# A two-layer hybrid diffusion backbone: modulation closes at raised priority, output-weight splits at a shorter spacing, half an output tile ahead of the last attention unit's close

## The chip, the cores and the metric

The kernel runs on one core of a Trainium2 chip. The metric is the device time of one execution in microseconds (us). The core has five engines that run side by side, each through its own queue of instructions: TensorE (PE; its weight loads are listed apart as PEld), VectorE (DVE), ScalarE (ACT), GpSimd (POOL) and SyncE (SP), which issues all of this kernel's DMAs. Semaphores order work between engines.

## What is computed

The reference is two layers over 1024 latent and 256 context tokens of width 1024. Each layer modulates a normalised input, projects it once, sends the columns through three groups of heads, and joins them in one output projection:

```
mod = silu(c) @ w_ada[l] + b_ada[l]              # shift, scale, gate
h   = rmsnorm(x, norm_g) * (1 + scale) + shift   # the same for the context
... = split(h @ w_in)
a   = gated delta rule, both directions, 4 heads of 128   # recurrence over tiles
b   = softmax attention, 4 heads, 10 key tiles of 128     # latent reads context + latent
c   = short gated convolution
x   = x + gate * (concat(a, b, c) @ w_out)       # the context too in the first layer
```

After the second layer only the 1024 latent tokens remain, and a last RMSNorm gives the output.

## The kernel before

Tokens are cut into ten tiles of 128 (eight latent, two context). Matrix products whose operands need more than one float32r pass are written as hi and lo parts, so a product is three passes: hi x hi, lo x hi, hi x lo. `split` (L74) makes such a pair: ScalarE copies the raw tile into hi, VectorE or POOL subtracts it to give lo.

**Order of the work.** Two things set it. First, the program issues its instructions through a small planner, `Sched` (L86): generators ("lanes") yield a delay, and `tick` moves the planner's clock and resumes the lanes that are due. The clock is advanced by estimates in the code, for example `sch.tick(0.0014 * n)` after each score product of n columns. `until(cond)` ticks by 1.0 until a condition holds. Second, the compiler then schedules each engine's queue by priority, which follows the order of issue, and by a model of when operands are ready; `tc.high_priority(offset=k)` issues as if k instructions earlier. Between L1279 and L1456, `tc.manual_schedule` keeps PE's instructions in the order of issue; the other engines stay free, and PE work issued after the region may still be placed between.

**Buffers.** Tiles come from tagged pools with a fixed number of buffers (L55). The change touches `P2` (7 buffers: `wr`, `ot2`, `za`, `zb`, `tm` and others), `T5` (5: `probT`, `xt`), `P4` and `B16` (7 large ones: among them the two halves of the output weights).

**Modulation.** `Ada` (L177) loads `w_ada`, multiplies it with the conditioning column, and `close` (L197) copies the product out of PSUM on ScalarE into `ms`, lets PE sum it over partitions (L209), and adds bias and scale on VectorE into A2 and B2 (L216, L218), which every modulated tile `hm` (L280) reads. For the first layer the closes stand at the very start; the others run as a lane beside the input projection.

**Attention.** The loop over `units` (group of queries, pair of heads) does five steps of two key tiles each (one step for the context group). A step issues scores (`a_scores`), exponentials into `probT` on ScalarE, sums of `probT` into `vt` on POOL (L1129; the last step's on VectorE, L1127, for the first head, and for both in the last unit), and the product with the values (`a_pv`, L1159). `a_out` (L1162) closes a unit: PE sums `vt` over partitions (L1170, "sum product"), VectorE takes the reciprocal (L1173) and scales, POOL multiplies by the gate, SP writes `bx_d`.

**Output.** When both directions of the recurrence are done, the lane `load_wo` (L1311) loads the output weights in two column halves of eight slices of 128 rows each: per slice a buffer `wr`, a DMA, a delay, a `split`, a delay (`load_wo_half`, L1324). `finish(i)` (L1332) treats one tile of tokens in four stages: load `ot2`, `raw` and `za`; the norm's statistics and the scaling of `ot` (L1344 to L1349); four transposes (L1353), scaling (L1354) and the split into `mix`, with the load of `xt`; and the output product, two column halves of 24 matmuls each (L84), with residual and gate on VectorE. `ahead(q)` (L1388) moves tiles q-2, q-1 and q on by one stage. `ahead(0)` and `ahead(1)` are called inside the last attention units, `ahead(2)` after the last value product; then come the last close, and a loop that calls `ahead(q)` and the output product of tile q-3.

Of the kernel before, what the change touches and what calls it, by code (L numbers as in the profile page):

```python
# [10 lines left out]
ALU = mybir.AluOpType  # L11
# [17 lines left out]
def kernel(  # L29
# [39 lines left out]
    V, A, P, T, S = nc.vector, nc.scalar, nc.gpsimd, nc.tensor, nc.sync  # L69
# [8 lines left out]
    def copy_a(out, in_):  # L78
        A.activation(out=out, in_=in_, func=ACTF.Copy)  # L79
# [41 lines left out]
    sch = Sched()  # L121
# [55 lines left out]
    class Ada:  # L177
# [18 lines left out]

        def close(self, third, q, pm, brow=None):  # L197
            ms = st([128, 256], "sm", name="ms")
            copy_a(ms, pm[:, 0:256])
            yield 3.0  # L200
            pc = bank()
            if third == 2:
                T.matmul(pc[0:32, 0:256], lhsT=csum, rhs=ms, start=True, stop=True)
                V.tensor_tensor(out=brow, in0=pc[0:2, 0:256], in1=brow, op=ALU.add)
                S.dma_start(out=self.y["gate"][:, 256 * q:256 * q + 256], in_=brow)
                return
            p3 = pc[:, 0:4].rearrange("p (b t) -> p b t", b=2)
            for b in range(2):
                T.matmul(p3[:, b], lhsT=ms[:, 128 * b:128 * b + 128], rhs=csum[:, 0:2], start=True, stop=True)  # L209
            out = self.y["A2" if third else "B2"][:, :, 2 * q:2 * q + 2]  # L210
            cols = self.y["col"]

            def row(c0):
                return cols[:, c0 + 2 * q:c0 + 2 * q + 2].unsqueeze(1).to_broadcast([128, 2, 2])

            V.tensor_tensor(out=out, in0=p3.rearrange("p b t -> p t b"), in1=row(78 + 8 * third), op=ALU.add)  # L216
            if third:
                V.scalar_tensor_tensor(out=out, in0=out, scalar=1.0, in1=row(60), op0=ALU.add, op1=ALU.mult)  # L218

        def lane(self):  # L220
            todo = [(t, q, k4) for t in self.thirds for q in range(4) for k4 in range(2)]
# [94 lines left out]
    for l in range(DEPTH):  # L316
# [603 lines left out]
        if l == 0:  # L920
# [16 lines left out]
            for t in (0, 1):  # L937
                for hf in range(2):
                    pms = [bank(), bank()]
                    for k4 in range(2):  # L940
                        for j in range(2):
                            q = 2 * hf + j
# [381 lines left out]
        def load_wo_half(q, wh, wl):  # L1324
            for k in range(KD):
                wr = st([128, 512], "P2", name="wr")
                S.dma_start(out=wr, in_=w_out[l, 128 * k:128 * k + 128, 512 * q:512 * q + 512])
                yield 1.5
                split(wr, wh[:, k], wl[:, k], P if k % 2 else V)
                yield 1.5  # L1330

        def finish(i):  # L1332
            raw = st([128, KD, 128], "P4", name="raw")
            ot = st([128, 4, 128], "P2", name="ot2")
            za = st([128, 4, 128], "P2", name="za")
            S.dma_start(out=ot, in_=o_d[i])
            S.dma_start(out=raw[:, 4:6, :], in_=bx_d[:, :, i * 128:(i + 1) * 128].rearrange("b p t -> p b t"))
            S.dma_start(out=raw[:, 6:8, :], in_=cx_d[:, :, i * 128:(i + 1) * 128].rearrange("b p t -> p b t"))
            S.dma_start(out=za, in_=za_d[:, :, i * 128:(i + 1) * 128].rearrange("b p t -> p b t"))
            yield 3.0  # L1340
            so = st([128, 4], "st", name="so")
            jk = st([128, 128], "h5", name="jk4")
            for h in range(4):
                A.activation(out=jk, in_=ot[:, h], func=ACTF.Square, accum_out=so[:, h:h + 1])  # L1344
            V.scalar_tensor_tensor(out=so, in0=so, scalar=1.0 / 128, in1=s_2[:, :, i], op0=ALU.mult, op1=ALU.mult)
            P.tensor_scalar(so, so, 1.0, EPS, ALU.mult, ALU.add)
            P.tensor_tensor(so, so, nhalf[:, 0:4], ALU.pow)
            V.tensor_tensor(out=so, in0=so, in1=s_1[:, :, i], op=ALU.mult)
            V.tensor_tensor(out=ot, in0=ot, in1=bc(so, 128), op=ALU.mult)  # L1349
            yield 3.0  # L1350
            pt = bank()
            for h in range(4):
                T.transpose(pt[:, h * 128:(h + 1) * 128], ot[:, h], ident)  # L1353
            V.scalar_tensor_tensor(out=raw[:, 0:4, :], in0=pt.rearrange("p (h f) -> p h f", h=4), scalar=col[:, 74:75], in1=za,  # L1354
                                   op0=ALU.mult, op1=ALU.mult)
            mix = st([128, 2, KD, 128], "W8", F32R, name="mix")
            split(raw[:, 0:4], mix[:, 0, 0:4], mix[:, 1, 0:4])
            split(raw[:, 4:8], mix[:, 0, 4:8], mix[:, 1, 4:8], P)
            xt = load_x(l, i)
            done[i] = xt  # L1360
            yield 3.5
            for q in range(2):
                pw = bank()
                wh, wl = wo[q]
                mm3(pw, [(mix[:, a_, k], w_[:, k]) for a_, w_ in ((0, wh), (1, wh), (0, wl)) for k in range(KD)])
                cs = slice(512 * q, 512 * q + 512)
                tm = st([128, 512], "P2", name="tm")
                V.tensor_tensor(out=tm, in0=pw, in1=gates[0 if i < NX else 1][:, cs], op=ALU.mult)
                V.tensor_tensor(out=xt[:, cs], in0=xt[:, cs], in1=tm, op=ALU.add)
                if last:  # L1370
                    if q == 0:
                        sf = st([128, 2], "st", name="sf")
                    A.activation(out=tm, in_=xt[:, cs], func=ACTF.Square, scale=D ** -0.5, accum_out=sf[:, q:q + 1])
            if not last:
                S.dma_start(out=xs_d[i], in_=xt)
                return
            V.scalar_tensor_tensor(out=sf[:, 0:1], in0=sf[:, 0:1], scalar=EPS, in1=sf[:, 1:2], op0=ALU.add, op1=ALU.add)
            P.tensor_tensor(sf[:, 0:1], sf[:, 0:1], nhalf[:, 0:1], ALU.pow)
            for q in range(2):
                cs = slice(512 * q, 512 * q + 512)  # L1380
                V.scalar_tensor_tensor(out=xt[:, cs], in0=xt[:, cs], scalar=sf[:, 0:1], in1=gates[1][:, cs], op0=ALU.mult, op1=ALU.mult)
                S.dma_start(out=out[0, i * 128:(i + 1) * 128, cs], in_=xt[:, cs])
# [69 lines left out]
        Q.clear()  # L1452
        ahead(2)
        sch.tick(2.0)
        next(ending)
        in_order.__exit__(None, None, None)  # L1456
        sch.tick(1.8)
        sch.until(lambda: wof.ok(0))
        for q in range(3, n_act + 3):
            ahead(q)  # L1460
            next(fg[q - 3], None)
            if q < n_act + 2:
                sch.tick(10.4)
            if last:
                continue
            if q > n_act:
                zpre.append(split_w(zr))
            if n_act <= q < n_act + 2:
                zr = load_w(l + 1, O_ZA + 128 * (q - n_act))
            if q == n_act + 2:  # L1470
                wof.put(1)
            sch.add(h_lane(act[q - 3], l + 1))
# [76 lines left out]
```

## Time and profile before

| | us |
|---|---|
| median of 3 runs | 1717.27 (1715.24 to 1718.92) |
| profiled execution | 1723.55 |
| its span, first to last instruction | 1721.8 |
| PE busy | 1650.5 |
| DVE busy | 1101.9 |
| ACT busy | 758.8 |
| POOL busy | 646.3 |

The table is to be read by stages. The share of an engine is a mean over stages with different limits; the number to look for is where PE stands idle or runs at its lower clock (the granted clock is given as a share of full speed: 1.00 is 2.4 GHz, 0.50 is 1.2 GHz). In the timeline a row gives the start, the duration, the engine, the line, the operation with its output and inputs, and in brackets the idle time before it and what ended that. Layer 0 ends its attention at about 803 us of the span, layer 1 at about 1614 us.

### The profile page before, as it was taken

Reading aid. Unit: us, or ns where it says so; the run is one execution under the profiler, and the core shown is the slowest. Engines: PE = TensorE matmul, PEld = TensorE weight load, DVE = VectorE, ACT = ScalarE, POOL = GpSimd, SP = SyncE. Lnnn points to the kernel's source line nnn. Section 1 sums busy time; section 2 is a strip of 40 time slices with the busy share of each in tenths; the row PEclk is TensorE's granted clock in tenths of the full one; section 3 lists DMA queues with packets and bytes.
Section 4 is the critical chain, followed back from the end, with each engine's and each line's share of the span. In section 5 each row is a group of like instructions: output and inputs, shape, how many; then the busy total and the mean of one; then the engine's idle time right before and its main releaser. Section 6 shows DMA issues by size and latency. Waiting matters only on the chain.

```text
span 1721.8 us, 29896 instructions
## 1 busy us (share of the span) xinstructions
PE 1650.5 (96%) x10964; PEld 1316.9 (76%) x10964; DVE 1101.9 (64%) x2041; ACT 758.8 (44%) x1909; POOL 646.3 (38%) x848
## 2 busy tenths in 40 slices
PE   7999999999999999998999999999999989999998
PEld 5887888787887877764888887787778778776586
DVE  2534668878643767765565346689797377776664
ACT  4644565223444534344354435652245444434432
POOL 0520345321320456557331212544232136556731
PEclk8999999999999899999999999999999989999999
DMA  9332464753254755544443314556524465454551
GB/s 360 124 126 79 155 196 150 242 178 123 78 160 125 257 157 177 186 144 159 132 141 111 104 56 134 161 179 224 166 70 128 151 211 164 160 188 156 172 159 49
DMA packets 195403, 266.54 MB, mean 155 GB/s; under 512 B 50529, under 2 KB 115249, under 8 KB 195257
## 3 DMA queue, kind: packets, MB, share of 16 engines
q1 hardware_dynamic: 195256, 264.64, 47.8%
q8 instruction: 87, 1.43, 0.3%
q14 instruction: 60, 0.48, 0.1%
HBM read 182.71 MB, written 79.17 MB: 152 GB/s over the span
## 4 chain that ended last, share of the span: by engine, by line
PE 68%; DVE 10%; DMA 9%; issue 5%; ACT 3%; POOL 3%; SPq 1%; POOLq 0%; DVEq 0%; ACTq 0%
PE bank L452 26%; PE bank L84 22%; PE bank L1159 3%; PE bank L1236 2%; PE bank L1255 2%; PE bank L1249 2%; DVE pr L680 2%; PE bank L1254 2%; PE bank L1102 2%; DMA gcb<-row_d 2%; DVE Mb L681 1%; DMA wa<-in_w_ada_dram 1%; PE bank L1226 1%; DVE acc L466 1%; PE bank L516 1%
## 5 line engine op out<-in xcount | busy, mean ns | idle before, releaser
L452 PE MATMUL bank<-h_hi,w 128*128 128x512 f32 x1664 | 432.5, 403 | 2.4 <-DVE h_hi L283 2.4
L452 PEld LDWEIGHTS bank<-h_hi,w 128*128 128x128 f32 x1664 | 305.4, 190 | 74.6 <-issue 4.5
L452 PE MATMUL bank<-h_lo,w 128*128 128x512 f32 x832 | 217.7, 402 | 0.0
L452 PEld LDWEIGHTS bank<-h_lo,w 128*128 128x128 f32 x832 | 154.3, 189 | 37.0 <-issue 1.6
L466 DVE SCALAR_TENSOR_TENSOR acc<-pad,col,acc 128x1284 f32<-128x1284 f32 (+1 forms) x104 | 160.1, 1540 | 11.1 <-ACT acc L463 9.5
L1129 POOL TENSOR_TENSOR vt<-vt,probT 128x512 f32<-128x512 f32 x110 | 144.7, 1335 | 20.2 <-ACT probT L1143 19.5
L84 PE MATMUL bank<-wo_hi,mix 128*128 128x512 f32 x576 | 145.0, 402 | 1.8 <-ACT wo_hi L75 1.1
L1143 ACT ACTIVATE probT<-bank 128x512 f32<-128x512 f32 (+1 forms) x168 | 96.5, 590 | 98.2 <-PE bank L84 92.2
L84 PEld LDWEIGHTS bank<-wo_hi,mix 128*128 128x128 f32 x576 | 108.2, 191 | 28.6 <-ACT wo_hi L75 2.6
L76 DVE TENSOR_TENSOR w<-wr,w 128x1024 fp32r<-128x1024 f32 x52 | 66.6, 1283 | 93.3 <-ACT w L75 93.3
L1104 DVE TENSOR_REDUCE mx<-bank 128x1 f32<-128x512 f32 (+1 forms) x200 | 108.5, 585 | 10.9 <-PE bank L1102 9.7
L452 PE MATMUL bank<-h_c,w 128*128 128x256 f32 x816 | 109.7, 287 | 0.0
L452 PEld LDWEIGHTS bank<-h_c,w 128*128 128x128 f32 x816 | 102.2, 190 | 5.8 <-issue 3.7
L75 ACT ACTIVATE w<-wr 128x1024 fp32r<-128x1024 f32 x52 | 54.9, 1060 | 75.3 <-PE bank L452 56.3
L84 PE MATMUL bank<-qt,kh 97*128 97x512 f32 (+1 forms) x256 | 84.4, 411 | 3.5 <-ACT probT L1143 2.8
L1159 PE MATMUL bank<-probT,vt 128*64 128x512 f32 (+1 forms) x336 | 79.4, 594 | 0.0
L1232 POOL TENSOR_TENSOR ring<-ring,qx 128x512 f32<-128x512 f32 x32 | 40.9, 1277 | 92.7 <-DMA ring<-row_d 76.8
L680 DVE TENSOR_TENSOR pr<-L,Mb 128x31 f32<-128x31 f32 (+15 forms) x186 | 70.7, 380 | 4.6
L84 PE MATMUL bank<-wo_lo,mix 128*128 128x512 f32 x288 | 73.5, 395 | 0.0
L681 DVE TENSOR_TENSOR Mb<-Mb,pr 128x31 f32<-128x31 f32 (+15 forms) x186 | 68.6, 369 | 5.0
L617 POOL TENSOR_TENSOR gcb<-gcb,gc 128x1024 f32<-128x1024 f32 x20 | 44.5, 2231 | 62.7 <-DMA gcb<-row_d 36.8
L79 ACT ACTIVATE pad<-bank 128x512 f32<-128x512 f32 (+1 forms) x78 | 41.0, 531 | 54.1 <-PE bank L452 39.1
(310 smaller groups left out, 3225.2 us busy)
## 6 DMA issues: line engine op xcount, KB each, us to landing
wr<-in_w_blk_dram SPq DMA_DIRECT2D x52, 512.0 KB
wa<-in_w_ada_dram SPq DMA_DIRECT2D x32, 512.0 KB
gcb<-row_d SPq DMA_DIRECT2D x20, 512.0 KB
nn_d<-N SPq DMA_DIRECT2D x20, 512.0 KB
ring<-vr_d SPq DMA_DIRECT2D x40, 256.0 KB
ring<-nn_d SPq DMA_DIRECT2D x40, 256.0 KB
qk_d<-gcb SPq DMA_DIRECT2D x18, 512.0 KB
ring<-kt_d SPq DMA_DIRECT2D x36, 256.0 KB
```

Of the source, the lines that this page charges most:

```text
L75: A.activation(out=hi, in_=raw, func=ACTF.Copy)
L76: eng.tensor_tensor(out=lo, in0=raw, in1=hi.bitcast(F32), op=ALU.subtract)
L84: T.matmul(outp, lhsT=lh, rhs=rh, start=q == 0, stop=q == n - 1)
L452: T.matmul(pb[:, 0:n], lhsT=self.w[:, wi, k, :], rhs=hg[g][hi][:, k, :], start=q + k == 0, stop=q == 2 and k == KD - 1)
L466: V.scalar_tensor_tensor(out=acc[:, 2:hi], in0=pad[:, 2 + t - r:hi + t - r], scalar=col[:, ci:ci + 1], in1=acc[:, 2:hi], op0=ALU.mult, op1 ...
L617: P.tensor_tensor(gcb, gcb, bc(gc[:, i, :], 128), ALU.subtract)
L680: V.tensor_tensor(out=pv, in0=bc(L[:, 0:k, k], w), in1=N[:, k:k + 1, k:32].to_broadcast([128, k, w]), op=ALU.mult)
L681: V.tensor_tensor(out=N[:, 0:k, k:32], in0=N[:, 0:k, k:32], in1=pv, op=ALU.subtract)
L1104: V.tensor_reduce(mx[:, gk:gk + 1], pb[:, 0:n], AX.X, ALU.max)
L1129: P.tensor_tensor(acc, a0, a1, ALU.add)
L1143: A.activation(out=pts[r][:, kk, 0:n], in_=pb, func=ACTF.Exp)
L1159: T.matmul(u["po"][64 * r:64 * r + 64, 0:n], lhsT=vx[:, kt, hh * 64:hh * 64 + 64], rhs=pts[r][:, kk, 0:n], start=kt == keys[0], stop=kt == ...
```

## The change

Four edits are made together.

- In `Ada.close`, the copy `ms` and the two VectorE operations that write A2 and B2 are issued at a priority 200 instructions earlier. The branch for the gate (third 2) has only its copy raised.
- In `load_wo_half`, the delay between the load of a slice and its split goes from 1.5 to 1.0, and the one after it from 1.5 to 0.7.
- `finish` yields once more, between the two column halves of the output product.
- After the last value product, the wait for the weights (`until`) and the first column half of tile 0 are issued ahead of the last unit's close, inside the region in which PE keeps the order of issue. A tick of 1.8 goes. In the loop, tile 0 then needs one call for its second half, and every later tile two.

```diff
--- before.py
+++ after.py
@@ -196,7 +196,8 @@
 
         def close(self, third, q, pm, brow=None):
             ms = st([128, 256], "sm", name="ms")
-            copy_a(ms, pm[:, 0:256])
+            with tc.high_priority(offset=200):
+                copy_a(ms, pm[:, 0:256])
             yield 3.0
             pc = bank()
             if third == 2:
@@ -213,9 +214,10 @@
             def row(c0):
                 return cols[:, c0 + 2 * q:c0 + 2 * q + 2].unsqueeze(1).to_broadcast([128, 2, 2])
 
-            V.tensor_tensor(out=out, in0=p3.rearrange("p b t -> p t b"), in1=row(78 + 8 * third), op=ALU.add)
-            if third:
-                V.scalar_tensor_tensor(out=out, in0=out, scalar=1.0, in1=row(60), op0=ALU.add, op1=ALU.mult)
+            with tc.high_priority(offset=200):
+                V.tensor_tensor(out=out, in0=p3.rearrange("p b t -> p t b"), in1=row(78 + 8 * third), op=ALU.add)
+                if third:
+                    V.scalar_tensor_tensor(out=out, in0=out, scalar=1.0, in1=row(60), op0=ALU.add, op1=ALU.mult)
 
         def lane(self):
             todo = [(t, q, k4) for t in self.thirds for q in range(4) for k4 in range(2)]
@@ -1325,9 +1327,9 @@
             for k in range(KD):
                 wr = st([128, 512], "P2", name="wr")
                 S.dma_start(out=wr, in_=w_out[l, 128 * k:128 * k + 128, 512 * q:512 * q + 512])
-                yield 1.5
+                yield 1.0
                 split(wr, wh[:, k], wl[:, k], P if k % 2 else V)
-                yield 1.5
+                yield 0.7
 
         def finish(i):
             raw = st([128, KD, 128], "P4", name="raw")
@@ -1371,6 +1373,8 @@
                     if q == 0:
                         sf = st([128, 2], "st", name="sf")
                     A.activation(out=tm, in_=xt[:, cs], func=ACTF.Square, scale=D ** -0.5, accum_out=sf[:, q:q + 1])
+                if q == 0:
+                    yield
             if not last:
                 S.dma_start(out=xs_d[i], in_=xt)
                 return
@@ -1452,13 +1456,15 @@
         Q.clear()
         ahead(2)
         sch.tick(2.0)
+        sch.until(lambda: wof.ok(0))
+        next(fg[0])
         next(ending)
         in_order.__exit__(None, None, None)
-        sch.tick(1.8)
-        sch.until(lambda: wof.ok(0))
         for q in range(3, n_act + 3):
             ahead(q)
             next(fg[q - 3], None)
+            if q > 3:
+                next(fg[q - 3], None)
             if q < n_act + 2:
                 sch.tick(10.4)
             if last:
```

## Rows read from the trace of the kernel before

**Rows 1.** The page: busy time, share of the span and instructions of each engine.

```profile
PE 1650.5 (96%) x10964; PEld 1316.9 (76%) x10964; DVE 1101.9 (64%) x2041; ACT 758.8 (44%) x1909; POOL 646.3 (38%) x848
```

**Rows 2.** Waits of PE, 803 to 822 us: total us, times, longest us.

```profile
PE bank L1353 <- DVE ot L1349: 4.0, 3, 2.5
PE bank L84 <- ACT wo_hi L75: 1.1, 2, 0.9
```

**Rows 3.** Timeline of PE, layer 0: start, us, operation, [idle before <- releaser].

```profile
804.49 0.65 PE L1170 MATMUL bank<-vt,cst 128*64 128x256 f32 x4
...
807.11 4.58 PE L84 MATMUL bank<-wo_hi,mix 128*128 128x512 f32 x18 [0.67 <-ACT mix L75]
...
814.46 0.50 PE L84 MATMUL bank<-wo_hi,mix 128*128 128x512 f32 x1 [0.91 <-ACT wo_hi L75]
...
818.12 0.63 PE L1353 MATMUL bank<-cst,ot 128*128 128x128 f32 x4 [2.49 <-DVE ot L1349]
...
835.99 0.60 PE L1353 MATMUL bank<-cst,ot 128*128 128x128 f32 x4
```

**Rows 4.** Chain that ended last, 840 to 860 us: start, us, what.

```profile
848.67 11.21 PE bank L84 x48
```

**Rows 5.** Windows: us, busy of PE, PEld, DVE, ACT, POOL; clock, DMA, GB/s.

```profile
819.00:821.00 2.00, 2.00 (x6) 1.62 (x5) 2.00 (x4) 1.40 (x6) 1.43 (x2) 0.50 0.70 220
...
1616.00:1622.00 6.00, 4.24 (x12) 2.42 (x13) 5.33 (x7) 2.19 (x4) 3.37 (x2) 0.72 0.91 339
```

**Rows 6.** Timeline of PE, layer 1, end of attention.

```profile
1614.00 0.66 PE L1353 MATMUL bank<-cst,ot 128*128 128x128 f32 x4
1617.76 1.97 PE L1170 MATMUL bank<-vt,cst 128*64 128x512 f32 x2 [3.10 <-DVE vt L1127]
...
1644.70 0.60 PE L1353 MATMUL bank<-cst,ot 128*128 128x128 f32 x4
```

**Rows 7.** Timeline of SP, loads of the output weights.

```profile
806.88 2.10 SPq L1327 DMA_DIRECT2D wr<-in_w_out_dram  x2
...
1622.43 7.66 SPq L1327 DMA_DIRECT2D wr<-in_w_out_dram  x6
```

**Rows 8.** Timelines of DVE and ACT, layer 1, ahead of the output product.

```profile
1614.71 1.74 DVE L1127 TENSOR_TENSOR vt<-vt,probT 128x512 f32<-128x512 f32 x1 [4.85 <-POOL vt L1129]
1616.37 0.74 DVE L1354 SCALAR_TENSOR_TENSOR raw<-bank,col,za 128x512 f32<-128x512 f32 x1
1617.03 1.28 DVE L1127 TENSOR_TENSOR vt<-vt,probT 128x512 f32<-128x512 f32 x2
...
1617.14 1.15 ACT L75 ACTIVATE mix<-raw 128x512 fp32r<-128x512 f32 x2 [6.02 <-DVE raw L1354]
```

**Rows 9.** Timeline of POOL, both layers.

```profile
777.99 14.58 POOL L1129 TENSOR_TENSOR vt<-vt,probT 128x512 f32<-128x512 f32 x11
...
1591.40 1.29 POOL L76 TENSOR_TENSOR wo_lo<-wr,wo_hi 128x512 fp32r<-128x512 f32 x1
...
1606.77 9.12 POOL L1129 TENSOR_TENSOR vt<-vt,probT 128x512 f32<-128x512 f32 x7
```

**Rows 10.** Timelines of ACT, PEld and PE at the start.

```profile
28.72 1.05 ACT L262 ACTIVATE jk<-xt 128x1024 f32<-128x1024 f32 x1
...
29.75 0.37 ACT L79 ACTIVATE ms<-bank 128x256 f32<-128x256 f32 x1
...
30.18 0.93 PEld L209 LDWEIGHTS bank<-cst,ms 128*128 128x128 f32 x4 [0.16 <-ACT ms L79]
...
36.48 1.59 PE L84 MATMUL bank<-wm_hi,h_hi 128*128 128x368 f32 x4 [0.24 <-DVE h_hi L283]
```

**Rows 11.** Timelines of ACT and PE, layer 0, during the recurrence's last steps.

```profile
747.36 1.33 ACT L75 ACTIVATE wo_hi<-wr 128x512 fp32r<-128x512 f32 x2 [2.60 <-DMA wr<-in_w_out_dram]
...
749.76 0.50 PE L1102 MATMUL bank<-kh,qt 96*128 96x512 f32 x1 [1.07 <-ACT ring L1244]
...
750.80 0.73 PE L84 MATMUL bank<-qt,kh 97*128 97x512 f32 x2 [0.53 <-ACT ring L1244]
```

## Prediction

> **What bounds the kernel now.** I read the page's busy times first: TensorE (PE) is busy for 1650.5 us of the 1721.8 us span [rows 1]. So only stretches in which PE stands still or runs at its lower clock can pay, and the change can touch three of them: the end of attention in layer 0, the same place in layer 1, and the start. Next I read PE's waits and PE's timeline there.
>
> Layer 0: between 803 and 822 us PE waits 4.0 us for scaled `ot` tiles and 1.1 us for `wo_hi` [rows 2]. The timeline puts these in order [rows 3]: the output product starts at 807.11, 0.67 late for `mix`; at 814.46 it finds no weights for the second column half (0.91 of the 1.1), then waits 2.49 until 818.12. The transposes of the fourth tile follow at 835.99. Between 807.11 and 835.99 lie 96 products and one set of transposes. At the undisturbed pace, 48 products in 11.21 us [rows 4], they need 22.42 + 0.38 = 22.8 us; they took 28.9. So 6.1 us are lost: 3.6 standing still, and about 2.5 at a reduced pace, since the granted clock is 0.50 (the 1.2 GHz level) right after the wait [rows 5].
>
> Layer 1: after the first tile's transposes (1614.00 to 1614.66) PE stands for 3.10 us until 1617.76, for the last unit's sums `vt` [rows 6]. The fourth tile's transposes begin at 1644.70. The work between is 96 products (22.42), four sum products (about 1.0) and two sets of transposes (0.75), together 24.2 us; 30.0 passed. So 5.9 us are lost: 3.1 standing, the rest again slow (a mean clock of 0.72 over the 6 us from 1616 [rows 5], which is 3.4 us at the lower level).
>
> **The change, part by part.** All of it is made against the profiled execution, 1723.55 us in all with 1721.8 of span; the median of the runs is 1717.27, 0.4% below. I take the saving over as it is.
>
> Weight loads. `load_wo_half` is a lane of the program's planner, which moves in steps of 0.0014 x 512 = 0.72 for each score product. A wait of 1.5 costs three steps, 1.0 or 0.7 costs two or one, so a 128-row slice takes about 2.2 planner units where it took 4.3. Worked through the loops of the code: before, 10 of 16 slices are issued ahead of the last unit's last product in layer 0 and 7 in layer 1; after it 15 and 12. That agrees with the issues on SP, six late ones in layer 0 (the first two at 806.88) and nine in layer 1 (the last six from 1622.43) [rows 7]. They are late because `P2` has seven buffers, and with three tiles' `ot2` and `za` and one `zb` all seven are held until the first tile's transposes; slices issued earlier come ahead of those. So in layer 0 five of the six late slices go into attention, and the wait for weights at 814 to 818 has no cause left. The wait named for `ot` goes with it: PE stood at the third tile's transposes only because nothing else was left to do, and with both halves of tile 0 ready there are 48 products, 11.2 us, ahead of them.
>
> Half a tile ahead. Inside the region in which PE's order is fixed, 24 products (5.6 us) now stand before the last unit's sum products. In layer 0 this has a price: the sum products (0.65 us at 804.49 [rows 3]) filled a hole in which PE waits for `mix`; they now run after the 24, at full price. Layer 0 then gains 6.1 - 0.65 = 5.4 us at most. The least is 0.5 (the `wo_hi` waits of 1.1 go, the 2.49 wait and its slow clock stay, less 0.65). The last slice is still loaded late and the hole before `mix` gets longer, so I take 4.0.
>
> In layer 1 the products can fill the 3.10 us hole only if `mix` is there. VectorE runs one add of `vt` at 1614.71, after 4.85 us of waiting for POOL, and only then the scaling L1354 at 1616.37; ScalarE's `mix` starts at 1617.14 and takes 0.6 for its first part, so about 1617.75 [rows 8]. In this order the hole stays as long as it is, and with it the slow clock after it: 3.4 us at half speed, worth 1.7. What goes is the rest, 5.9 - 3.1 - 1.7 = 1.1 us. If L1354 goes first instead, `mix` is ready at about 1616.1 (1614.66 + 0.74 + 0.6 and hand-overs), the hole is halved, and if the clock then stays up the gain is up to 4.
>
> What the moved splits cost. Each slice is a ScalarE copy and a subtraction, half of them on POOL at 1.29 us [rows 9]. POOL is the full engine there: it adds `vt` back to back, 11 in 14.58 us in layer 0 and 7 in 9.12 us in layer 1 [rows 9]. Layer 1 moves three POOL subtractions ahead of the end (3.9 us at most), layer 0 two or three. Those scheduled behind the backlog of adds cost nothing; one that lands ahead delays `vt`, so the add on VectorE, L1354 behind it, and `mix`. I take 0.5 us in layer 1 between 0 and 3.9, so layer 1 gains 0.6 (from -2.8 to +4). DVE and ScalarE have room: ScalarE has 6.02 us idle ahead of `mix` [rows 8].
>
> The Trainium skill's page GPSIMD Engine Reference (section 1. Specifications) says that POOL shares its SBUF interfaces with VectorE and contends with VectorE instructions that read two SBUF inputs. The trace agrees: the `vt` add that ran beside POOL took 1.74 us, the next two 1.28 together [rows 8]. By that rule the three moved pairs would stretch each other by about 1 us each, 3 us, which is inside the range above.
>
> Modulation close. At the start the last `ms` copy on ScalarE (29.75) stands behind a square of 1.05 us. PE feels little of it: it waits 0.16 us for that copy (its weight load at 30.18) and 0.24 us at 36.48 for `h_hi`, which needs A2 [rows 10]; both may go, so 0.4 us (bounds 0 and 0.8: at most the copy's own delay of about 0.6, from the end of its product near 29.15, and the 0.24). The other closes run beside a full PE and are set at nothing; if one of these copies is put in front of its own product on ScalarE it costs a few tenths.
>
> **Sum.** 0.4 + 4.0 + 0.6 = 5.0 us: 1718.5 for such an execution, 1712.3 for the median. 0.2% of this kernel is 3.4 us, about what a measurement can tell from no change.
>
> **Rivals.**
> First, *the waits move into attention*. ScalarE takes its work in order; a split whose slice has not landed holds the exponentials behind it. At 747.36 it stood 2.60 us for a slice, and PE then lost 1.07 and 0.53 at 749.76 and 750.80 (the wait is put down to ScalarE) [rows 11]. Five more splits in each layer, if half of them cost 1 us, return 5 us: 1717. Against it: at the two layers' ends ScalarE is idle for long, and several such waits cost PE nothing. The Trainium skill's page TensorE: Matmul & The Clock Gate (section Architectural detail: the array is 16× 32×32, not 1× 128×128) states that ScalarE and VectorE are strict first-in, first-out; if every moved split held PE as the one at 747.36 did, 1.6 us each, ten would cost 16 us. The trace agrees with the order, not with that price.
>
> Second, *slower through POOL*. If the POOL subtractions land inside the saturated adds in both layers, 2 x 3 x 1.29 = 7.7 us of delay reach the last exponentials (the five `T5` buffers come free by POOL's adds) and the sum products. It decides from about 5 us on, where it eats the whole gain; in full, and with layer 1's hole as long as before, the kernel is 2 to 3 us slower, 1720. Against it: adds have the earlier place in the order.
>
> Third, *the better order in layer 1* (L1354 first, no slow clock): 3.4 us more, 1709.
>
> Fourth, *the change doesn't reach*: the pool of seven still holds the slices back, or PE keeps waiting for `ot` in layer 0. Then only 0.5 + 0.6 + 0.4 remain: 1716.
>
> **How the numbers follow.** Forecast 0.45, third rival 0.15, first and fourth together 0.27, second 0.13. Faster by over 0.2%: nearly all of the forecast and the third, 0.57. Within 0.2%: the first and the fourth and the forecast's edge, 0.30. Slower: 0.13. The range 1706.5 to 1718.5 reaches from both layers at their best with the start (5.4 + 4 + 0.8 = 10.2, so 1707, and half a microsecond) to just above the first rival; it leaves most of the second out.
>
> **What would show it.** Right: in layer 0 no PE wait for `wo_hi`, and about 24 us instead of 28.9 from the first output product to the fourth tile's transposes; in layer 1 the output product directly after the hole, the sum products behind 24 of them, and some 29 us instead of 30. Wrong: new PE waits for `probT` between 735 and 800 or 1566 and 1612, POOL's last `vt` add later against PE's last attention product than before, or a clock of 0.50 after a longer hole ahead of `mix` in layer 0.

## The result and the profile after

The changed kernel takes 1737.27 us in the median of 7 runs (1734.66 to 1741.37); the kernel before, run beside it, 1717.55. The ratio is 1.0106, 95% interval 1.0087 to 1.0124. By the ratio the change costs about 18 us (the two medians differ by 19.7); the forecast was 5.0 us less than before, 1712.3.

The profiled execution took 1741.37 us, its span 1739.6, 17.8 more than before. The busy times of its page (columns as in [rows 1]):

```profile
PE 1653.7 (95%) x10964; PEld 1316.8 (76%) x10964; DVE 1102.0 (63%) x2041; ACT 759.8 (44%) x1909; POOL 651.3 (37%) x848
```

PE does 3 us more of busy time and so stands idle about 15 us longer. Starts of single instructions in both traces cut the span into stretches. A "value product" is `a_pv`'s (L1159 before, L1161 after; line numbers after `close` are higher by 2 in the changed kernel). The differences are taken before rounding.

| stretch, us | before | after | difference |
|---|---|---|---|
| start to first value product, layer 0 | 606.2 | 607.7 | +1.5 |
| first to last value product, layer 0 | 196.5 | 199.6 | +3.1 |
| last value product to fourth tile's transposes, layer 0 | 33.3 | 29.2 | -4.2 |
| from there to first value product, layer 1 | 595.4 | 596.5 | +1.1 |
| first to last value product, layer 1 | 182.0 | 185.2 | +3.1 |
| last value product to fourth tile's transposes, layer 1 | 31.2 | 44.5 | +13.2 |
| from there to the end | 77.1 | 77.1 | 0 |

The output's start in layer 0 came as forecast. Both attentions and above all layer 1's end lost time. The first stretch and the fourth moved by as much from kernel to kernel where nothing in them was edited, so nothing is read from them.

**Layer 0**, timeline of PE (start, us, operation, idle before and what ended it), to be held against [rows 3]:

```profile
811.67 2.15 PE L84 MATMUL bank<-wo_hi,mix 128*128 128x512 f32 x8 [2.54 <-ACT mix L75]
814.12 2.13 PE L84 MATMUL bank<-wo_hi,mix 128*128 128x512 f32 x8 [0.30 <-DVE mix L76]
...
818.05 0.65 PE L1172 MATMUL bank<-vt,cst 128*64 128x256 f32 x4
...
836.39 0.60 PE L1355 MATMUL bank<-cst,ot 128*128 128x128 f32 x4
```

There is no wait for `wo_hi` and none for the third tile's `ot`. From the first output product to the fourth tile's transposes 24.7 us pass; before it was 28.9.

**Layer 1**, timeline of PE, to be held against [rows 6]:

```profile
1618.60 0.66 PE L1355 MATMUL bank<-cst,ot 128*128 128x128 f32 x4
1624.49 6.11 PE L84 MATMUL bank<-wo_hi,mix 128*128 128x512 f32 x16 [5.24 <-ACT mix L75]
1630.44 2.03 PE L84 MATMUL bank<-wo_lo,mix 128*128 128x512 f32 x8
1632.39 1.08 PE L1172 MATMUL bank<-vt,cst 128*64 128x512 f32 x4
1633.40 0.66 PE L1355 MATMUL bank<-cst,ot 128*128 128x128 f32 x4
1633.81 3.98 PE L84 MATMUL bank<-wo_hi,mix 128*128 128x512 f32 x16
1637.64 2.03 PE L84 MATMUL bank<-wo_lo,mix 128*128 128x512 f32 x8
1649.01 1.11 PE L1355 MATMUL bank<-cst,ot 128*128 128x128 f32 x4 [9.34 <-DVE ot L1351]
...
1662.55 0.60 PE L1355 MATMUL bank<-cst,ot 128*128 128x128 f32 x4
```

From the end of the first transposes (1619.26) to the fourth set 43.3 us pass, 30.0 before, for the same 24.2 us of work: 5.2 and 9.3 us of standing, and 4.5 at reduced pace. The windows right behind the two holes show that pace (columns as in [rows 5]; the clock is third from the end):

```profile
1624.50:1629.50 5.00, 5.00 (x12) 3.96 (x13) 3.36 (x4) 1.66 (x3) 2.95 (x2) 0.53 0.96 324
...
1649.00:1653.00 4.00, 3.99 (x12) 3.32 (x13) 2.30 (x4) 0.63 (x1) 0.00 (x0) 0.50 0.43 133
```

The second hole is new. PE waits for the scaling (L1351) of the third tile, tile 2. ScalarE's timeline and then VectorE's say why it is late:

```profile
1633.33 1.27 ACT L75 ACTIVATE wo_hi<-wr 128x512 fp32r<-128x512 f32 x2 [5.50 <-DMA wr<-in_w_out_dram]
1638.14 0.64 ACT L75 ACTIVATE mix<-raw 128x512 fp32r<-128x512 f32 x1 [3.54 <-DVE raw L1356]
1639.75 0.63 ACT L75 ACTIVATE mix<-raw 128x512 fp32r<-128x512 f32 x1 [0.97 <-PE bank L84]
1640.28 0.61 ACT L1375 ACTIVATE tm<-xt 128x512 f32<-128x512 f32 x1
1640.80 0.18 ACT L1375 ACTIVATION_READ_ACCUMULATOR tm<-xt 128x1 f32 x1
1640.90 0.29 ACT L1346 ACTIVATE jk<-ot 128x128 f32<-128x128 f32 x1
```

```profile
1644.87 1.41 DVE L1385 SCALAR_TENSOR_TENSOR xt<-xt,sf,gate_c 128x512 f32<-128x512 f32 x2 [0.67 <-POOL sf L1382]
1646.20 0.23 DVE L1347 SCALAR_TENSOR_TENSOR so<-so,s 128x4 f32<-128x4 f32 x2
...
1648.26 0.69 DVE L1351 TENSOR_TENSOR ot<-ot,so 128x512 f32<-128x512 f32 x1
```

The load of tile 2 is not the reason: SP issued it at 1606.78, and in i_stats_first (below) the statistics followed the same load by 3 us. In ScalarE's queue tile 2's statistics (L1346, 1640.90) stand behind splits whose slices landed late, behind both parts of tile 1's `mix`, and behind the square of tile 0's first half (L1375), which needs the half's 24 products. They are done at 1642.2, but VectorE takes them up (L1347) only at 1646.20, after it has closed the whole of tile 0: its second half and its last norm (L1385). In the kernel before, the scaling of three tiles was done ahead of the end of attention (timeline of DVE, before):

```profile
1592.74 1.75 DVE L1349 TENSOR_TENSOR ot<-ot,so 128x512 f32<-128x512 f32 x1
...
1602.73 0.71 DVE L1349 TENSOR_TENSOR ot<-ot,so 128x512 f32<-128x512 f32 x1
1606.84 1.24 DVE L1348 TENSOR_TENSOR so<-so,s 128x4 f32<-128x4 f32 x1 [3.41 <-POOL so L1347]
1608.12 1.74 DVE L1349 TENSOR_TENSOR ot<-ot,so 128x512 f32<-128x512 f32 x1
```

After, only tile 0's is done by then. Tile 1's comes at 1621.82, after the last value product, and what stands behind it keeps the first hole open (DVE, and POOL beside it):

```profile
1611.89 9.89 DVE L1350 TENSOR_TENSOR so<-so,s 128x4 f32<-128x4 f32 x1 [6.92 <-POOL so L1349]
1621.82 0.69 DVE L1351 TENSOR_TENSOR ot<-ot,so 128x512 f32<-128x512 f32 x1
...
1623.03 0.74 DVE L1356 SCALAR_TENSOR_TENSOR raw<-bank,col,za 128x512 f32<-128x512 f32 x1
```

```profile
1611.82 9.94 POOL L1131 TENSOR_TENSOR vt<-vt,probT 128x512 f32<-128x512 f32 x8
```

A product of 128x4 lasted as long as eight of POOL's adds, and tile 0's L1356, on which `mix` waits, was queued behind it, behind the scaling and behind one add of `vt`.

### The profile page after: what moved, and what is told of

The parts are those of the page before. It is cut to its first block, busy times and chain, and to the rows that moved or that the text cites. A ratio compares the mean times of both kernels' runs of the same rounds, so it can differ in the third digit from the quotient of the medians.

```text
span 1739.6 us, 29917 instructions
## 1 busy us (share of the span) xinstructions
PE 1653.7 (95%) x10964; PEld 1316.8 (76%) x10964; DVE 1102.0 (63%) x2041; ACT 759.8 (44%) x1909; POOL 651.3 (37%) x848
## 4 chain that ended last, share of the span: by engine, by line
PE 50%; DVE 9%; DMA 5%; issue 4%; ACT 2%; POOL 2%; SPq 1%; DVEq 0%; POOLq 0%; ACTq 0%
PE bank L84 19%; PE bank L454 13%; PE bank L1161 3%; PE bank L1238 2%; PE bank L1257 2%; PE bank L1251 2%; PE bank L1256 2%; PE bank L1104 2%; PE bank L1228 1%; DVE pr L682 1%; DVE Mb L683 1%; DVE mx L1106 1%; DMA tt<-blk_o 1%; DMA gcb<-row_d 1%; PE bank L518 1%
## 5 line engine op out<-in xcount | busy, mean ns | idle before, releaser
L76 DVE TENSOR_TENSOR w<-wr,w 128x1024 fp32r<-128x1024 f32 x52 | 65.8, 1267 | 91.5 <-ACT w L75 90.9
L1161 PE MATMUL bank<-probT,vt 128*64 128x512 f32 (+1 forms) x336 | 81.0, 605 | 0.0
L707 POOL COPY N<-tt 32x256 f32<-32x256 f32 x80 | 56.4, 704 | 27.7 <-DMA tt<-blk_o 24.8
```

The costliest lines, as they stand in the source:

```text
L76: eng.tensor_tensor(out=lo, in0=raw, in1=hi.bitcast(F32), op=ALU.subtract)
L707: P.tensor_copy(out=N[r, :, :, r], in_=nd[r])
L1161: T.matmul(u["po"][64 * r:64 * r + 64, 0:n], lhsT=vx[:, kt, hh * 64:hh * 64 + 64], rhs=pts[r][:, kk, 0:n], start=kt == keys[0], stop=kt == ...
```

## The experiments

Ratios are to the kernel before, run on the same chip. The other columns are read from each trace as in the table above: last value product to fourth tile's transposes in layer 0 ("out 0"); first to last value product in layer 1 ("att 1"); last value product to fourth transposes in layer 1 ("out 1"); and when the scaling of tile 2 began, against layer 1's last value product. All in us.

| kernel | ratio, 95% interval | out 0 | att 1 | out 1 | tile 2 scaled |
|---|---|---|---|---|---|
| before | 1 | 33.3 | 182.0 | 31.2 | -5.4 |
| changed | 1.0106, 1.0087 to 1.0124 | 29.2 | 185.2 | 44.5 | +30.2 |
| e1_close | 0.9995, 0.998 to 1.001 | 33.3 | 179.3 | 32.4 | -5.4 |
| e2_spacing | 1.0023, 1.0007 to 1.0039 | 27.6 | 184.8 | 34.9 | +0.1 |
| e3_half | 1.0076, 1.0055 to 1.0097 | 33.8 | 180.7 | 42.7 | +30.3 |
| e5_spacing_half | 1.0104, 1.0088 to 1.0121 | 27.9 | 185.3 | 44.7 | +30.3 |
| g_close_first | 1.0116, 1.0094 to 1.0137 | 27.8 | 185.4 | 43.5 | +28.5 |
| f1_so_pool | 1.0117, 1.0077 to 1.0157 | 31.7 | 184.7 | 44.8 | +30.9 |
| g_prep_first | 1.0034, 1.002 to 1.0048 | 28.7 | 185.9 | 32.6 | +0.1 |
| i_stats_first | 1.005, 1.0033 to 1.0067 | 27.9 | 187.5 | 33.5 | +0.1 |
| j_lead | 1.0061, 1.004 to 1.0082 | 30.4 | 188.1 | 35.2 | +0.1 |
| k_sub_v | 1.0035, 1.0017 to 1.0052 | 29.0 | 186.6 | 32.1 | -0.9 |
| l_first4_old | 1.0007, 0.999 to 1.0023 | 29.7 | 179.7 | 34.7 | -1.1 |
| h_ab_l0 | 0.9992, 0.9981 to 1.0004 | 26.9 | 179.5 | 31.7 | +2.0 |
| j_lead_l0 | 1.001, 0.9988 to 1.0032 | 26.3 | 180.8 | 31.8 | -5.2 |
| n_l0_first4 | 0.9998, 0.9983 to 1.0013 | 29.5 | 180.6 | 31.4 | -5.4 |

**The parts by themselves.** Four runs stand between two theories: that POOL's adds, unbroken once the splits are moved, hold VectorE, and that the close, issued behind the half tile, comes too late. The raised closes alone (the two writes of A2 and B2 in the same way):

```diff
-            copy_a(ms, pm[:, 0:256])
+            with tc.high_priority(offset=200):
+                copy_a(ms, pm[:, 0:256])
...
```

> Only the raised priority of the modulation close; weight spacing and the end of attention are as in the kernel before. Both theories of the loss put it at the layers' ends: the first (POOL's moved splits make its run of adds unbroken, and VectorE stands beside it) and the second (the sum products and the reciprocal now come 24 products later, and all VectorE work behind them with it). By both this kernel shows the start alone: PE 1.2 to 1.4 us earlier from 40 us on, and a ratio to the kernel before of 0.998 to 1.001. A ratio above 1.005 would mean that the close itself disturbs later stages, and both would be wrong in part.

0.9995: nothing that can be measured.

The shorter spacing alone:

```diff
-                yield 1.5
+                yield 1.0
                 split(wr, wh[:, k], wl[:, k], P if k % 2 else V)
-                yield 1.5
+                yield 0.7
```

> Only the shorter spacing of the weight splits. By the first theory (POOL) most of the loss is here: a small VectorE product stands 5 to 10 us beside POOL's adds at the end of layer 1, the first tile's mix is 5 us late, ratio 1.004 to 1.008. By the second (order of the close) layer 1 ends as in the kernel before, layer 0 gains 3 to 4 us, the ratio is 0.997 to 1.000.

1.0023, between the ranges of the two theories: out 0 falls by 5.7 us, but layer 1's attention and its end give back 2.8 and 3.7.

The half tile ahead alone (with the yield in `finish` and the two calls in the loop), and the same with the spacing:

```diff
         sch.tick(2.0)
+        sch.until(lambda: wof.ok(0))
+        next(fg[0])
         next(ending)
...
```

> Only the half tile ahead of the last close, with the old spacing: all splits are then issued ahead of the first half. By the second theory the loss is here: the third tile's transposes in layer 1 wait 8 to 12 us for the scaled ot, ratio 1.005 to 1.010. By the first it is not: no VectorE product over 3 us beside POOL, ratio 0.999 to 1.003.

> Spacing and half tile together, without the raised close: the changed kernel less its start. By both theories the whole loss at the ends is here: PE 13 us later over the start of layer 1's output stage, ratio 1.010 to 1.013. If the ratio is under 1.005, the loss hangs on how the schedule falls and on no single edit.

The half tile alone has nearly all of layer 1's loss (42.7 against 31.2), with no VectorE instruction held beside POOL there: tile 1's scaling took 1.74 us. So POOL is not the main cause, and the loss came with the half tile. But the wait that was expected, for the third tile's `ot`, is not in this trace. PE's waits from 1618 to 1662 us of e3_half (total, times, longest) are others:

```profile
PE bank L84 <- ACT wo_hi L75: 4.9, 5, 1.6
PE bank L84 <- ACT mix L75: 4.3, 1, 4.3
```

At the old spacing the weights come too late for a tile 0 that is taken first; in the changed kernel they are there, and the wait for tile 2 stands in their place. With the spacing (e5_spacing_half) it is the changed kernel, with and without the raised closes.

**What in the half tile costs.** Three theories for layer 1's end: the place of the close (A), VectorE held beside POOL (B), or the half's place ahead of the next tiles' preparation (C). Each of the three edits is made on the changed kernel; in the third, the loop skips its own `ahead(3)`:

```diff
-        next(fg[0])
         next(ending)
+        next(fg[0])
         in_order.__exit__(None, None, None)
```

> The changed kernel with one swap: the last unit's close (sum products, reciprocal) is issued ahead of the first half of tile 0 again, both still inside the region that keeps PE's order. In the changed kernel layer 1 takes 113.6 us from the last value product to the last output product, 100.4 before; 5.2 us of it are a wait for mix of tile 0 and 9.3 a wait for the scaled ot of the third tile. Theory A (place of the close: the sum products behind 24 products make the 3.4 us reciprocal late, and what stands behind it on VectorE): the 9.3 us wait shrinks below 3, the 5.2 stays, the stretch takes about 105 us and the kernel is some 8 us faster than the changed one (about 1729, ratio to before 1.006). Theory B (VectorE held beside POOL's unbroken adds): the 5.2 stays, 113 us. Theory C (the half tile is issued before the next tiles are prepared, so PE has nothing to take): 9.3 us stays, 113 us, ratio 1.010.

```diff
-            V.tensor_tensor(out=so, in0=so, in1=s_1[:, :, i], op=ALU.mult)
+            P.tensor_tensor(so, so, s_1[:, :, i], ALU.mult)
```

> The changed kernel with the 128x4 product that scales so (L1350) moved from VectorE to POOL, next to the two POOL operations ahead of it, so that VectorE has no small product to be held beside POOL's eight adds (9.89 us in the changed kernel). Theory B (POOL holds VectorE): the hole of 5.2 us ahead of tile 0's output product falls to about 2 or less with the slow clock after it, the stretch in layer 1 takes 106 to 109 us instead of 113.6, ratio to before about 1.006. Theories A and C: at most the 5.2 us hole changes, the 9.3 us wait and its slow clock stay: 110 us or more, ratio 1.008 or above. If POOL takes the product only behind its adds, ot comes as late as before and nothing changes (1.0104).

```diff
         sch.until(lambda: wof.ok(0))
+        ahead(3)
         next(fg[0])
         next(ending)
...
```

> The changed kernel with the next step of tiles 1, 2 and 3 (ahead(3): transposes of tile 1, statistics of tile 2, loads of tile 3) issued ahead of the half tile instead of behind it; the half tile still stands ahead of the close. Theory C (preparation behind the half tile is what PE lacks): the 9.3 us wait for the third tile's ot is gone or below 2 us, the stretch in layer 1 falls from 113.6 to 103 to 105 us, ratio to before about 1.005. Theory A (place of the close): the reciprocal still comes behind 24 products, so the stretch stays near 111 us, ratio 1.009. Theory B: the wait for mix of tile 0, 5.2 us, is as long as before or longer, and nothing else changes.

A falls as the main cause: with the close ahead of the half again, out 1 is still 43.5. PE's wait for tile 2 is shorter there, 5.1 us instead of 9.3, but 7.6 us instead of 4.5 go to reduced pace, and 5.4 of standing for `vt` take the place of 5.2 for `mix`. f1_so_pool did not take B's hold away: with the product gone from VectorE, the next instruction, the scaling of 128x512, was held instead, and PE's waits are as large. Both are in these lines (DVE; then PE's waits 1618 to 1668: total, times, longest), of f1_so_pool:

```profile
1618.57 7.88 DVE L1351 TENSOR_TENSOR ot<-ot,so 128x512 f32<-128x512 f32 x1 [8.32 <-POOL so L1350]
```

```profile
PE bank L1355 <- DVE ot L1351: 10.3, 1, 10.3
PE bank L84 <- ACT mix L75: 4.9, 1, 4.9
```

B falls as the main cause by other kernels: e3_half has the loss without a hold, and h_ab_l0 (below) has a hold of 8.65 us, there of tile 2's product and until 2.0 us after the last value product, and not the loss, with out 1 at 31.7 (DVE):

```profile
1598.92 8.65 DVE L1350 TENSOR_TENSOR so<-so,s 128x4 f32<-128x4 f32 x1 [3.42 <-POOL so L1349]
```

C holds: with `ahead(3)` issued first, out 1 is back to 32.6 and tile 2 is scaled at +0.1 instead of +30.2. `ahead(3)` moves three tiles, so the next run moves only tile 2's second stage and leaves tiles 1 and 3 to the loop:

```diff
         sch.until(lambda: wof.ok(0))
+        next(fg[2])
         next(fg[0])
         next(ending)
...
```

> The changed kernel with one step moved: the statistics and scaling of the third tile (the second stage of finish for tile 2) are issued ahead of the half tile; the transposes of tile 1 and the loads of tile 3 stay behind it, and so does the close. Theory C1 (ScalarE and VectorE, in order, reach the third tile's statistics only behind the work that waits for tile 0's first half): three tiles are scaled ahead of the end of attention, as before the change; PE's wait of 9.3 us for the third tile's ot in layer 1 is gone, the stretch from the last value product to the last output product is 102 to 105 us instead of 113.6, ratio to before 1.003 to 1.005. Theory C2 (tile 1's transposes behind the half are what PE lacks): the stretch stays at 110 us or more, ratio 1.009.

33.5 us, tile 2 scaled at +0.1. Timeline of PE of this kernel:

```profile
1617.64 0.66 PE L1355 MATMUL bank<-cst,ot 128*128 128x128 f32 x4
1620.34 2.82 PE L84 MATMUL bank<-wo_hi,mix 128*128 128x512 f32 x8 [2.05 <-ACT mix L75]
1625.45 3.44 PE L84 MATMUL bank<-wo_hi,mix 128*128 128x512 f32 x8 [2.29 <-DVE mix L76]
...
1650.63 0.60 PE L1355 MATMUL bank<-cst,ot 128*128 128x128 f32 x4
```

The half tile is still ahead of the close, tile 1's transposes are still behind it; the hole of 9.3 is gone, 11 of the 13.2 us are back, and the kernel is at 1.005. Tile 1's product is not held in this kernel, but the first hole is now two, 2.05 and 2.29 us, so less than 1 us of the 11 comes from there. What was moved is tile 2's place in the program; which of the instructions that it was moved past held it most (the square, the splits, tile 1's `mix`, the last norm) was not tried singly. In the table all kernels that scale tile 2 some 30 us late have out 1 between 42.7 and 44.8 (e3_half by the other waits shown above), all others 31.2 to 35.2.

**What the spacing costs.** In every kernel with the short spacing from the first slice in layer 1, att 1 is 184.7 to 188.1; in all others 179.3 to 182.0. ScalarE and PE in the changed kernel:

```profile
1574.03 1.28 ACT L75 ACTIVATE wo_hi<-wr 128x512 fp32r<-128x512 f32 x2 [2.74 <-DMA wr<-in_w_out_dram]
1575.22 2.16 ACT L1246 ACTIVATE ring<-bank,bco 128x128 f32<-128x128 f32 x8
```

```profile
1576.40 0.50 PE L1104 MATMUL bank<-kh,qt 96*128 96x512 f32 x1 [2.64 <-ACT ring L1246]
1577.44 0.80 PE L84 MATMUL bank<-qt,kh 97*128 97x512 f32 x2 [0.54 <-ACT ring L1246]
```

Two more splits than before stand ahead of the recurrence's last copies (L1246); ScalarE waits 2.74 us for their slices, and PE for the copies. Three ways to take that away were tried, all on the kernel with the spacing alone. An earlier load (`slab` holds the two lines taken out):

```diff
+            nx = slab(0)
             for k in range(KD):
-                wr = st([128, 512], "P2", name="wr")
-                S.dma_start(out=wr, in_=w_out[l, 128 * k:128 * k + 128, 512 * q:512 * q + 512])
+                wr = nx
                 yield 1.0
+                nx = slab(k + 1) if k + 1 < KD else None
                 split(wr, wh[:, k], wl[:, k], P if k % 2 else V)
                 yield 0.7
```

> The kernel before with the shorter spacing alone, and each slice's load issued one slice earlier, ahead of the split of the slice before it. In the run with the spacing alone layer 1's attention (first to last value product) took 184.8 us against 182.0 before and 179.3 to 180.7 in the other runs with the old spacing, layer 0's 201.4 against 196.5 to 199.6; PE waited there 2.5 and 0.5 us for ScalarE's ring copies, which stood behind a split whose slice had not landed. Theory L (ScalarE waits for the slices): these two waits go, layer 1's attention falls to about 181 us, and the ratio to before from 1.0023 to about 1.000. Theory P (the subtractions on POOL push its adds back): the two waits may go, but attention stays within 1 us of the run with the spacing alone, ratio 1.002.

A miss: att 1 is 188.1 and the ratio 1.0061. SP still issued the four slices from 1565.85 on, over 5.3 us (6.1 with the spacing alone), and waited 3.6 of them for one of POOL's subtractions (L76), which frees a `wr`: the load waits for a free buffer, not for its place in the program.

All subtractions on VectorE:

```diff
-                split(wr, wh[:, k], wl[:, k], P if k % 2 else V)
+                split(wr, wh[:, k], wl[:, k], V)
```

> The kernel before with the shorter spacing alone, and all subtractions of the output weights' splits on VectorE, none on POOL. Theory P (POOL's subtractions push its adds of vt back, and with them the sum products): the last add comes earlier, the stretch in layer 1 falls from 104.1 back to 100 to 101 us, and attention loses 1 to 3 us less in each layer: ratio about 0.999 instead of 1.0023. Theory L (ScalarE waits for slices): layer 1's PE waits of 2.5 and 0.5 us for the ring copies stay, attention there stays near 185 us, ratio 1.001 to 1.002.

Out 1 falls from 34.9 to 32.1, so 2.8 of the 3.7 us that the spacing loses at layer 1's end are POOL's subtractions. The whole is no faster, 1.0035; both theories had expected less. Att 1 is 186.6 although PE's waits for the ring copies are gone here: PE waits 2.2 us for `probT` and 0.6 for VectorE instead.

The first four slices at the old spacing:

```diff
-                yield 1.0
+                yield 1.0 if q or k > 3 else 1.5
                 split(wr, wh[:, k], wl[:, k], P if k % 2 else V)
-                yield 0.7
+                yield 0.7 if q or k > 3 else 1.5
```

> The kernel before with the shorter spacing from the fifth slice on; the first four slices keep the old spacing, so that in both layers ScalarE has the same splits ahead of the recurrence's last ring copies as before the change. In the runs with the spacing alone ScalarE stood 2.55 us for a slice in front of these copies, and PE 2.5 and 0.5 us for them. Theory L (the early splits hold the copies): these PE waits are as before, layer 1's attention is back from 184.8 to 180 to 182 us; the gain at the start of layer 0's output stays (about 125 to 126 us instead of 131), ratio to before between 0.998 and 1.000. Theory P (any split more in attention costs POOL or ScalarE time that PE gives): attention in layer 1 stays at 184 us or more, ratio 1.002.

Att 1 is back to 179.7, and no wait for the ring copies is left. Out 1 stays at 34.7, the POOL part, and the ratio, 1.0007, cannot be told from 1. So the short spacing of the first four slices is the cause of the loss in layer 1's attention. The waits for the copies are the way that it takes in the changed kernel, and not the only one, as the run before this shows.

**Is there a better version?** The closes and the spacing in layer 0 alone, the same with the earlier load, and the same from the fifth slice on:

```diff
-                yield 1.0
+                yield 1.5 if last else 1.0
                 split(wr, wh[:, k], wl[:, k], P if k % 2 else V)
-                yield 0.7
+                yield 1.5 if last else 0.7
```

> The kernel before with the raised closes and, in layer 0 alone, the shorter spacing of the output weights; no half tile ahead. If the spacing's cost in layer 1 (3.7 us at its end, about 3 in its attention, as the run with the spacing alone shows) is separate from its gain in layer 0 (5.8 us at the end of attention against about 3 in it), this is 3 us faster than before, and the start's 1.4 may add to it: ratio 0.997 to 0.9985. If every split moved into attention costs about what it saves, 0.9995 to 1.001.

> The kernel before with the raised closes, the shorter spacing in layer 0 alone, and each slice's load issued one slice earlier in both layers. If the earlier load takes ScalarE's waits for slices away, layer 0 keeps its 5.8 us at the end of attention and gives back less than 1 us in it, and layer 1 is not disturbed: 4 to 6 us faster than before, ratio 0.9965 to 0.998. If not, it is as the same kernel without the earlier load, 0.9992.

> The kernel before with the raised closes, and the shorter spacing in layer 0 alone and from the fifth slice on. By theory L layer 0 gains 5 us at the start of its output and loses under 1.5 us in attention, layer 1 is undisturbed: ratio to before 0.9965 to 0.9985. By theory P it is as with the shorter spacing on all of layer 0's slices, 0.9992.

0.9992, 1.001 and 0.9998: none is shown to be faster than the kernel before, though all keep layer 1 whole and gain 3.8 to 7.0 us of out 0. Layer 0's attention, 196.5 to 199.6 us with the old spacing in both layers (before, e1_close, e3_half), took 200.6 to 206.0 in these three, so it gives back at least 1 us and perhaps all of the gain. Which of its waits does it was not settled.

## Why the prediction was wrong

**The half tile in layer 1 is the step that failed.** Layer 1's end was set at a gain of 0.6 us between -2.8 and +4 (1.1 for the half tile, less 0.5 for POOL), and lost 13.2; the half tile alone lost 11.5 (e3_half). That is 13.8 of the 22.8 us between the forecast and the profiled span. The working looked at where the 24 products stand in PE's order and whether `mix` is there. It did not ask what stood behind them in the program: `next(fg[0])` was moved ahead of `ahead(3)`, so what waits for the half on VectorE and ScalarE (L1370, L1371, the square L1375) came ahead of tile 2's statistics and scaling. In the kernel before, layer 1's end had rested on three tiles scaled in advance, and no row of that was among those read. Moving that one stage of tile 2 back returned 11 us (i_stats_first). The term itself was not far off: with the preparation first, out 1 is 33.5 and 32.6 (i_stats_first, g_prep_first) against 34.9 with the spacing and no half tile, 1.4 and 2.3 us less in single traces.

PE's order made it dearer. Tile 1's `mix` was complete at 1642.70 (its last subtraction, on POOL, started at 1640.99 and took 1.71), but tile 2's transposes, at 1649.01, stood ahead of tile 1's products: some 6.3 of the 9.34 us had work waiting.

**The first hole** did not stay at 3.1 but grew to 5.2. The prediction put `mix` late for the order L1127 ahead of L1354. In the changed kernel the held product of tile 1 stood ahead of both (until 1621.78). It isn't the only thing that can keep this hole open: in e3_half, with no hold, three adds of L1127 ahead of L1354 made it 4.3 us.

**Layer 0's output start** was right in size and cause: 4.0 taken, 4.2 measured in the changed kernel, no wait for `wo_hi`, 24.7 us instead of "about 24". The hole before `mix` grew to 2.54, as the prediction allowed. The half tile has no part in the gain: the spacing alone gave 5.7. Nor did it do the harm of layer 1 there: tile 2's scaling in layer 0 began 15.5 us after the last value product, 14.6 before. In both kernels ScalarE waited there for the load of tile 2's `ot` (until 811.65 before, 816.03 after), so no statistics done in advance could be lost. Layer 0 has no square and no last norm behind the output product either; what that is worth was not tried.

**The first rival came true beside the forecast**, in layer 1 as described: ScalarE in order, a split whose slice has not landed, PE 2.6 and 0.5 us late. It had been priced at 5 us for both layers; att 0 and att 1 gave 3.1 each in the profiled pair. The cause is shown for layer 1 only; layer 0's 199.6 us are still within what the kernels with the old spacing took (196.5 to 199.6). The Trainium skill's page TensorE: Matmul & The Clock Gate (section Architectural detail: the array is 16× 32×32, not 1× 128×128) states that ScalarE is strictly first-in, first-out; the rows agree with that. The 16 us that the prediction worked out for the case that every split is dear did not come.

**POOL's subtractions** were taken as 0.5 us in layer 1 between 0 and 3.9; the end of layer 1 shows 2.8 (e2_spacing against k_sub_v): inside the bounds, and over five times the value. The second rival built on them is still not the cause: it would have given 1720.

**The closes**: 0.4 forecast, nothing measured. The raised priority did not change the order: ScalarE's last `ms` copy (29.96) still stands behind the square of 1.05 us (28.92), and PE starts the product that it had waited for at 36.68 where it was 36.48 [rows 10], after 0.76 us for `h_hi`. PE is 1.4 us ahead by 50 us in the changed kernel, but that is the clock: it was granted 1.00 from 30 to 40 us, 0.50 before. e5_spacing_half, without raised closes, had 1.00 and the same lead; n_l0_first4, with them, had 0.50 and next to none.

**The signs named in advance**: the sum products stand behind 24 products, as said, and yet the stretch took 43 us and not 29; POOL's last add of `vt` ended 3.7 us after the last value product, before 2.4. In layer 0 the clock stayed up behind the longer hole (1.00 from 811.7 to 816.7), and in layer 1's attention the new waits were for the ring copies and not for `probT` (1.3 us, before 1.4 and 0.3). No rival was slower by more than 3 us, because none followed the half tile along the order of ScalarE's and VectorE's work on the next tiles.

## What to carry to other kernels

When a block is issued earlier, list everything that it is moved past, on every engine: its consumers move up in the other engines' queues too, and there they wait for the block itself. Preparation of the next tiles belongs ahead of such a block. A load or split that is pulled forward should be set against the next copy in the same queue that the critical engine needs, and a saving at one place is to be counted only after both layers have been looked at for that.

## What the runs showed of the hardware

A small VectorE instruction can stand for a whole run of POOL's: 128x4 took 9.89 us beside eight adds that follow one another (9.94 in all), and 0.16 later in the same trace, at 1648.06; 128x512 took 9.13 (g_close_first) and 7.88 (f1_so_pool) instead of 0.69. It happens with the old spacing too, and need not cost anything: 8.65 and 7.91 in h_ab_l0 and j_lead_l0, layer 1, with out 1 at 31.7 and 31.8. In the kernel before, the same product, beside POOL's seven adds [rows 9], was done beside the first of them, in 1.24 us. The Trainium skill's page SBUF — State Buffer (section SBUF: two separate sides) states that the port pair that the two engines share is locked for a whole instruction by the one that starts first, where VectorE reads two SBUF inputs, as here, and POOL reads SBUF too. The trace agrees with that for one add; why VectorE is let in after one add in some kernels and after eight in others is in no row read here and stays open.

PE's clock fell to the 1.2 GHz level behind both holes (0.53 and 0.50 in the windows above), so 14.6 us of standing cost some 4.5 us more in the work after it.
